# Strassen's scheme in the second matmul of a feed-forward network: seven block products in place of eight

## The chip, the cores and the metric

The kernel runs on one core of a Trainium2 chip. It is timed in device microseconds (us) for one whole execution; less is better. A core has TensorE (PE, matmuls out of the on-chip memory SBUF into the accumulators of PSUM), VectorE (DVE), ScalarE (ACT), GpSimd (POOL) and a queue, SP, that issues the DMAs here. Each engine works through its own list of instructions in the listed order and waits for the others by semaphores.

## The reference

One encoder layer on 2048 tokens of width 1024, in float32. The change concerns its last third:

```python
x = x + rms_norm(mix, g_post_mix)
h = rms_norm(x, g_pre_ffn)
f = jnp.square(jax.nn.relu(h @ w_ff1)) @ w_ff2      # 1024 -> 4096 -> 1024
return x + rms_norm(f, g_post_ffn)
```

## The kernel before

Three stages follow each other: the input projection, attention with the gating unit, and `stage3` (L889), which holds the output projection and the feed-forward network. Matmuls keep float32 accuracy by a split of every operand into a high part (`wh`, `fh`, `hh`, made by ACT) and a rest (`wl`, `fl`, `hl`, made by DVE as operand minus high part); `mm3` (L90 to L94) then takes three matmuls for one product: high by rest, rest by high, high by high. `split_sbuf` (L50 to L60) is the pair of instructions for a source in SBUF: ACT writes `hi` (L59, or L56 with a gain), DVE reads source and `hi` from SBUF and writes `lo` (L60, or L57 with the gain).

The network runs in two halves of 1024 tokens. A half goes through eight groups `g` of 512 hidden units. For a group, `ff1_unit` (L935) makes two of the group's four 128-unit blocks at a time, for both 512-token parts: PE sums over eight pieces of `w1` into four PSUM banks `f0` to `f3`; ACT takes the relu out of PSUM (L954), POOL squares it (L955), ACT and DVE split it into `fh` and `fl` (L59, L60). Then `ff2` (in `stage3`) multiplies the four blocks with the group's eight pieces of `w2` (4 rows of 128 by 2 columns of 512). It takes four PSUM banks at a time, each a 128-token by 512-column part of the result, sums four products of 128 hidden units into each, and DVE adds the bank to the sum `acc` in SBUF (L1083; ACT copies it in a half's first group, L1081). In the last group `done` adds the residual and writes out.

All weight halves share a pool of eight buffers `wh` and eight `wl` (`c.wp`): `w2` pieces take the place of `w1` pieces that FF1 has used, and `w1` pieces for the next group take the place of used `w2` pieces. Raw weights arrive through three buffers `wraw`. PSUM has six banks for products (`pm`) and two for transposes.

Outside the output projection (which is listed by hand, `in_order`) the order on each engine is made by the framework's scheduler when the kernel is built: it plans with its own estimates, and the engines then follow that list.

Of the kernel before, what the change touches and what calls it, by code (L numbers as in the profile page):

```python
# [9 lines left out]
F32 = mybir.dt.float32  # L10
F32R = mybir.dt.float32r
# [78 lines left out]
def mm3(nc, out, lh, ll, rh, rl, start=False, stop=False):  # L90

    nc.tensor.matmul(out, lhsT=lh, rhs=rl, start=start, stop=False)  # L92
    nc.tensor.matmul(out, lhsT=ll, rhs=rh, start=False, stop=False)  # L93
    nc.tensor.matmul(out, lhsT=lh, rhs=rh, start=False, stop=stop)  # L94
# [794 lines left out]
def stage3(tc, c, a, out):  # L889
# [4 lines left out]
    with ExitStack() as ctx:  # L894
        cst = ctx.enter_context(tc.tile_pool(name="s3c", bufs=1))
        hp = ctx.enter_context(tc.tile_pool(name="s3h", bufs=1))
        wk = ctx.enter_context(tc.tile_pool(name="s3k", bufs=2))
        sm = ctx.enter_context(tc.tile_pool(name="s3s", bufs=4))
        pm = ctx.enter_context(tc.tile_pool(name="s3p", bufs=6, space=PSUM))
# [4 lines left out]
        x1d = [dr.tile([1024, D], F32, name=f"x1d{e}", tag=f"x1d{e}") for e in range(2)]  # L904
# [8 lines left out]

        def normed(x1, out):
            rs = meansq(x1)
            nc.scalar.activation(out, x1, AF.Copy, scale=rs)
# [10 lines left out]
        def new_h():  # L927
            hh = hp.tile([P, 8, 1024], F32R, name="hh3", tag="hh3")
            hl = hp.tile([P, 8, 1024], F32R, name="hl3", tag="hl3")
            return hh, hl  # L930

        h = new_h()
        fpa = ctx.enter_context(tc.tile_pool(name="s3f", bufs=2))

        def ff1_unit(h, ws, c0, es, fs, pool):  # L935

            hh, hl = h
            bs = [pm.tile([P, 512], F32, name=f"f{m}", tag="mm3") for m in range(2 * len(es))]
            for kc in range(8):
                wh, wl = ws[kc]  # L940
                for m, b in enumerate(bs):
                    k, e = divmod(m, len(es))
                    cs = slice(c0 + k * P, c0 + (k + 1) * P)
                    ts = slice(es[e] * 512, (es[e] + 1) * 512)
                    mm3(nc, b, wh[:, cs], wl[:, cs], hh[:, kc, ts], hl[:, kc, ts], kc == 0, kc == 7)
                yield
            for k in range(2):
                if len(fs) == k:
                    fs.append(tuple(pool.tile([P, 1024], F32R, name=x, tag=x) for x in ("fh", "fl")))
                fh, fl = fs[k]  # L950
                for e in range(len(es)):
                    ts = slice(es[e] * 512, (es[e] + 1) * 512)
                    sq = wk.tile([P, 512], F32, name="sq", tag="sq")
                    nc.scalar.activation(sq, bs[k * len(es) + e], AF.Relu)  # L954
                    nc.gpsimd.tensor_tensor(sq, sq, sq, ALU.mult)  # L955
                    split_sbuf(nc, sq, fh[:, ts], fl[:, ts])

        def load2(g):
            return [[piece(nc, c, w2[(4 * g + k) * P:(4 * g + k + 1) * P, n * 512:(n + 1) * 512]) for k in range(4)]
                    for n in range(2)]  # L960

        with ExitStack() as octx:
# [9 lines left out]
            def load_x(i):  # L972
                xt = wk.tile([P, D], F32, name="xt3", tag="xt3", bufs=3)
                nc.sync.dma_start(xt, x2[i * P:(i + 1) * P, :])
                return xt
# [14 lines left out]
            raws, ws0, fs0, fs1 = [], [], [], []  # L990
            early = {7: 3, 8: 3, 9: 3, 11: 3, 12: 2, 13: 2, 14: 2}
            for i in range(18):
                old = 0 <= i - 1 < 16
                if 0 <= i - 3 < 8:
                    turned(xs[i - 3], h[0], h[1], i - 3)
                if i + 1 < 16:
                    halves(i + 1)
                if 0 <= i - 2 < 16:
                    nc.sync.dma_start(x1d[(i - 2) // 8][((i - 2) % 8) * P:((i - 2) % 8 + 1) * P, :], parts[i - 2])
                    if i - 2 < 8:  # L1000
                        rs2 = meansq(parts[i - 2])
# [6 lines left out]
                if i in (7, 11):  # L1008
                    unit = ff1_unit(h, ws0, 0, (i // 11,), fs0, fpa)
                for n in range(2):  # L1010
# [12 lines left out]
                    if 0 <= i - 2 < 8 and n == 1:  # L1023
# [14 lines left out]
        v0 = load2(0)  # L1038
        fpb = ctx.enter_context(tc.tile_pool(name="s3g", bufs=2))
        for _ in ff1_unit(h, ws0, 256, (0, 1), fs1, fpb):  # L1040
            pass

        gpost = bcast_row(nc, cst, a["g_post_ffn"][0:1], D, "gpost", "gain")
        with ExitStack() as fctx:
            ap_ = fctx.enter_context(tc.tile_pool(name="s3a", bufs=1, side="right"))

# [4 lines left out]
            def ff1(h, ws):  # L1051
                fs = []
                for pr, pool in enumerate((fpa, fpb)):
                    two = []
                    for _ in ff1_unit(h, ws, 2 * pr * P, (0, 1), two, pool):
                        pass
                    fs += two
                return fs

            def ff2(fs, ws, acc, first, last, done):  # L1060
                groups = [[(n, 4 * q + m) for m in range(4)] for n in range(2) for q in range(2)]
                if last:
                    groups = [[(n, m) for m in range(2) for n in range(2)]] + [[(n, m) for n in range(2)] for m in range(2, 8)]
                for grp in groups:
# [165 lines left out]
```

## Time and profile before

| | |
|---|---|
| median of three runs | 2489.77 us (2485.67 to 2494.03) |
| the profiled execution's own time | 2489.89 us |
| its span, first to last instruction | 2488.1 us |
| PE, DVE, ACT, POOL busy | 96%, 43%, 38%, 19% of the span |
| instructions of PE, DVE, ACT, POOL | 11591, 2262, 2069, 521 |
| feed-forward network alone | about 1100 to 2480 us, PE busy in every slice |

In the profile a group of instructions is given with its line, engine, operation, output and inputs, the shape and the count. A row of the timeline gives start, duration (of the whole row, where it merges several), engine, line, operation and, in brackets, how long the engine was idle before it and what ended that. A busy span of PE counts a matmul until its modelled end, so starts are compared with starts here.

### The profile page before, as it was taken

To read this page: it belongs to the slowest core of one execution; us is meant where nothing else is said; L and a number is where in the kernel's file an instruction comes from. 1 tells how busy PE (TensorE), PEld (TensorE's weight loads), DVE (VectorE), ACT (ScalarE), POOL (GpSimd) and SP (SyncE) were. 2 spreads that over 40 slices of the span, in tenths; PEclk is the share of its full clock that TensorE was granted. 3 is DMA by queue.
4 is the path that set the end of the run, shared out by engine and by line. 5 is a ranking of instruction groups with operands and counts; after the bars stand their busy time and mean duration, and the time that the engine had idled before them with its cause. 6 is when DMAs were issued, how large, how long until landed. Compare 5 with 4: busy or idle time off the path is not lost.

```text
span 2488.1 us, 31513 instructions
## 1 busy us (share of the span) xinstructions
PE 2385.7 (96%) x11591; PEld 1993.2 (80%) x11591; DVE 1072.5 (43%) x2262; ACT 934.0 (38%) x2069; POOL 463.3 (19%) x521
## 2 busy tenths in 40 slices
PE   7999999998889997899999999999999999999998
PEld 6787887887778876788888888888788888888887
DVE  5433523577766644751332332233622233223226
ACT  4424422377767774532221222123533122212212
POOL 4103102533222222320010011001211001001101
PEclk9999999999989998999999999999999999999999
DMA  7646365888867567761111111111611111111113
GB/s 271 218 140 203 119 188 160 216 199 191 197 170 179 144 173 223 228 230 38 58 46 46 55 52 49 37 60 57 206 55 47 46 56 51 47 39 55 47 47 118
DMA packets 213886, 296.13 MB, mean 119 GB/s; under 512 B 37090, under 2 KB 120549, under 8 KB 210661
## 3 DMA queue, kind: packets, MB, share of 16 engines
q1 hardware_dynamic: 188196, 280.23, 37.4%
q10 hardware_dynamic: 22976, 9.71, 1.5%
q0 software_dynamic: 2560, 4.20, 1.2%
q8 instruction: 91, 1.49, 0.3%
q14 instruction: 63, 0.51, 0.1%
HBM read 216.04 MB, written 82.74 MB: 120 GB/s over the span
## 4 chain that ended last, share of the span: by engine, by line
PE 64%; DMA 7%; DVE 3%; ACT 3%; POOL 1%; issue 1%; ACTq 0%; SPq 0%; DVEq 0%; POOLq 0%
PE f L92 10%; PE f L93 10%; PE f L94 10%; PE g L94 8%; PE g L93 8%; PE g L92 8%; PE t L599 1%; PE o L628 1%; PE o L627 1%; DMA yd<-x1b 1%; PE s L515 1%; DMA x1b<-stb 1%; PE s L516 1%; DMA od<-av 1%; PE mo L92 1%
## 5 line engine op out<-in xcount | busy, mean ns | idle before, releaser
L92 PE MATMUL g<-wl,fh 128*128 128x512 f32 x1024 | 398.8, 389 | 0.0
L94 PE MATMUL g<-wh,fh 128*128 128x512 f32 x1024 | 398.6, 389 | 0.0
L93 PE MATMUL g<-wh,fl 128*128 128x512 f32 x1024 | 398.6, 389 | 0.0
L93 PE MATMUL f<-hh,wl 128*128 128x512 f32 x1024 | 398.5, 389 | 0.0
L94 PE MATMUL f<-hh,wh 128*128 128x512 f32 x1024 | 398.5, 389 | 0.0
L92 PE MATMUL f<-hl,wh 128*128 128x512 f32 x1024 | 398.3, 389 | 0.0
L955 POOL TENSOR_TENSOR sq<-sq 128x512 f32<-128x512 f32 x128 | 132.0, 1051 | 1158.0 <-ACT sq L954 1142.8
L56 ACT ACTIVATE wh<-wraw,gain 128x512 fp32r<-128x512 f32 x200 | 143.3, 724 | 519.3 <-PE g L94 423.2
L57 DVE SCALAR_TENSOR_TENSOR wl<-wraw,gain,wh 128x512 fp32r<-128x512 f32 x200 | 157.7, 796 | 273.5 <-ACT wh L56 271.0
L60 DVE TENSOR_TENSOR fl<-sq,fh 128x512 fp32r<-128x512 f32 x128 | 99.5, 777 | 385.8 <-ACT fh L59 377.0
L93 PEld LDWEIGHTS f<-hh,wl 128*128 128x128 f32 x1024 | 192.2, 188 | 40.1
L92 PEld LDWEIGHTS f<-hl,wh 128*128 128x128 f32 x1024 | 192.2, 188 | 40.0
L94 PEld LDWEIGHTS f<-hh,wh 128*128 128x128 f32 x1024 | 192.2, 188 | 40.0
L93 PEld LDWEIGHTS g<-wh,fl 128*128 128x128 f32 x1024 | 192.3, 188 | 39.8
L94 PEld LDWEIGHTS g<-wh,fh 128*128 128x128 f32 x1024 | 192.2, 188 | 39.8
L92 PEld LDWEIGHTS g<-wl,fh 128*128 128x128 f32 x1024 | 192.2, 188 | 39.6
L1083 DVE TENSOR_TENSOR acc<-g,acc 128x512 f32<-128x512 f32 x192 | 127.3, 688 | 165.1 <-PE g L94 165.1
L588 ACT ACTIVATE p<-p,m 128x256 f32<-128x256 f32 (+2 forms) x384 | 173.9, 458 | 32.8 <-DVE m L558 15.7
L954 ACT ACTIVATE sq<-f 128x512 f32<-128x512 f32 x128 | 74.8, 597 | 285.4 <-PE f L94 278.4
L60 DVE TENSOR_TENSOR wl<-wraw,wh 128x512 fp32r<-128x512 f32 x136 | 93.9, 691 | 166.4 <-ACT wh L59 165.2
L59 ACT CAST wh<-wraw 128x512 fp32r<-128x512 f32 x136 | 84.6, 622 | 179.3 <-PE f L94 167.4
L532 DVE CUSTOM_DVE_ANT_0 p<-s,bias 128x256 f32<-128x256 f32 (+2 forms) x384 | 121.3, 356 | 44.3 <-PE s L516 31.6
(166 smaller groups left out, 4169.1 us busy)
## 6 DMA issues: line engine op xcount, KB each, us to landing
wraw<-in_w_ff_dram SPq DMA_DIRECT2D x256, 256.0 KB, 2.7
wraw<-in_w_in_dram SPq DMA_DIRECT2D x72, 256.0 KB, 2.9
xt<-in_x_dram SPq DMA_DIRECT2D x32, 512.0 KB, 6.6
v<-vd SPq DMA_DIRECT2D x40, 256.0 KB, 6.0
v<-vd SPq DMA_DIRECT2D x8, 1088.0 KB, 6.5
hd<-ht ACTq DMA_DIRECT2D x16, 512.0 KB, 4.7
vd<-vt SPq DMA_DIRECT2D x16, 512.0 KB, 3.1
qd<-e SPq DMA_DIRECT2D x32, 256.0 KB, 2.8
```

The source lines that it names most:

```text
L56: nc.scalar.activation(hi, src, AF.Copy, scale=scale)
L57: nc.vector.scalar_tensor_tensor(lo, src, scale, f32(hi), ALU.mult, ALU.subtract)
L59: nc.scalar.copy(hi, src)
L60: nc.vector.tensor_tensor(lo, src, f32(hi), ALU.subtract)
L92: nc.tensor.matmul(out, lhsT=lh, rhs=rl, start=start, stop=False)
L93: nc.tensor.matmul(out, lhsT=ll, rhs=rh, start=False, stop=False)
L94: nc.tensor.matmul(out, lhsT=lh, rhs=rh, start=False, stop=stop)
L532: nc.vector.tensor_tensor_reduce(po, so, bo, -1.0, 1e38, ALU.add, ALU.min, o.nm[:, br, cc:cc + 1])
L588: nc.scalar.activation(p[:, at + lo:at + hi], p[:, at + lo:at + hi], AF.Exp, bias=o.m[:, br, cc:cc + 1], scale=-1.0, accum_out=o.dn[:, br, ...
L954: nc.scalar.activation(sq, bs[k * len(es) + e], AF.Relu)
L955: nc.gpsimd.tensor_tensor(sq, sq, sq, ALU.mult)
L1083: nc.vector.tensor_tensor(av, b, av, ALU.add)
```

## The change

Only the network changes. Tokens go in four passes of 512 (`ps`) in place of two halves of 1024, and within a group of 512 hidden units the second matmul is done by Strassen's scheme in Winograd's form. The 512 tokens are two blocks of 256, the 1024 output columns two blocks of 512, the 512 hidden units two blocks of 256 (each as two parts `p` of 128). Seven products stand where eight block products stood; each is made for two token tiles `m` and takes two parts of three matmuls. So a group has 14 units of 6 matmuls, 84 matmuls for 512 tokens, where the kernel before has 192 for 1024. Over the run the second matmul has 2688 matmuls, before 3072; the first has 3072 in both.

What is new beside the products:

- `squares` (POOL): the relu stays in one buffer for each hidden block and is squared in two instructions of 128x256.
- `operands`: for each part, four POOL instructions on 128x256 make the sums of token blocks (`s1`, `s2`, and two in place), and seven splits (ACT L59, DVE L60, 128x256) make `fh1` to `fh7` and `fl1` to `fl7`.
- `load2`, `differences`, `second2`: `w2` comes in rows of 1024 columns (512 KB); eight POOL instructions on 128x512 make the differences of column blocks, and 14 splits of 128x512 make the weights of the products (before 8). The weights of products 1, 2, 6 and 5 have a pool of their own (`w2p`); those of 7, 3 and 4 go into `c.wp`.
- `CHAIN`: products 6, 7 and 4 go on summing into the bank `k=1` of product 1, product 3 into the bank of product 5. Between two of them DVE has to add the bank's present sum to a part of `acc` (L1154): 14 additions a group for 512 tokens, before 16 for 1024. `mm3` passes on a flag for banks that are continued.
- Each group of `w1` and `w2` is loaded and split once a pass, so four times instead of twice.

```diff
+        def squares(b, m, raw):
+            raw[m] = fp.tile([P, 512], F32, name="rf", tag=f"rf{m}")
+            nc.scalar.activation(raw[m], b, AF.Relu)
+            for e in range(2):
+                sl = raw[m][:, 256 * e:256 * e + 256]
+                nc.gpsimd.tensor_tensor(sl, sl, sl, ALU.mult)
...
+        def differences(raws):
+            ts = []
+            for r1, r2 in raws:
+                t1 = fp.tile([P, 512], F32, name="t1", tag="t1", bufs=2)
+                t2 = fp.tile([P, 512], F32, name="t2", tag="t2", bufs=2)
+                nc.gpsimd.tensor_tensor(t1, r1[:, 512:], r1[:, :512], ALU.subtract)
+                nc.gpsimd.tensor_tensor(t2, r2[:, 512:], t1, ALU.subtract)
+                nc.gpsimd.tensor_tensor(r1[:, 512:], r2[:, 512:], r1[:, 512:], ALU.subtract)
...
+            def operands(raw, p, fs):
+                a11, a21 = raw[p][:, :256], raw[p][:, 256:]
+                a12, a22 = raw[p + 2][:, :256], raw[p + 2][:, 256:]
...
+                nc.gpsimd.tensor_tensor(s1, a21, a22, ALU.add)
+                nc.gpsimd.tensor_tensor(s2, s1, a11, ALU.subtract)
+                op(1, a11)
+                op(2, a12)
+                op(6, s2)
+                op(5, s1)
+                nc.gpsimd.tensor_tensor(a21, a11, a21, ALU.subtract)
+                op(7, a21)
+                nc.gpsimd.tensor_tensor(a12, a12, s2, ALU.subtract)
+                op(3, a12)
+                op(4, a22)
...
+            CHAIN = ((1, 1, 0, 0, True, True, False), (2, 0, 0, 0, True, False, True), (6, 1, 0, 1, False, True, False),
+                     (5, 2, 1, 1, True, True, False), (7, 1, 1, 1, False, False, True),
+                     (3, 2, 0, 1, False, False, True), (4, 1, 1, 0, False, True, True))
...
+                order = [(x, m) for x in CHAIN for m in range(2)]
                 if last:
+                    order.sort(key=lambda x: x[1])
+                for j, ((n, k, r, q, opens, one, end), m) in enumerate(order):
+                    b = banks[k][m]
+                    ts = slice(m * P, (m + 1) * P)
+                    for p in range(2):
+                        fh, fl = fs[n, p]
+                        mm3(nc, b, fh[:, ts], fl[:, ts], *ws[n, p], opens and p == 0, p == 1, not opens)
+                    i = m + 2 * r
+                    av = acc[:, i, q * 512:(q + 1) * 512]
+                    if first and one:
+                        nc.scalar.copy(av, b)
+                    else:
+                        nc.vector.tensor_tensor(av, b, av, ALU.add)
...
                 for g in range(NG):
+                    first2(v, w2s)
+                    if not ps == g == 0:
+                        for _ in ff1_first(h, ws, raw):
+                            pass
+                        for _ in ff1_one(h, ws, 2, raw):
+                            pass
+                    operands(raw, 0, fs)
+                    for _ in ff1_one(h, ws, 3, raw):
+                        pass
+                    operands(raw, 1, fs)
...
+                    second2(v, w2s)
+                    if not last or ps < 3:
                         ws = load1((g + 1) % NG)
...
+                    ff2(fs, w2s, acc, g == 0, last, done, between)
```

How the scheduler lists these on the engines is shown at three places, all in one group (pass 1, fifth group) where the first matmul ends and the products begin. 24 of the 32 groups are listed like this; the last group of a pass differs only from the last row of the second place on (its products are ordered by token tile, and the very last group has no `w1` left to split), the first group of a pass somewhat more (ACT copies the banks of products 1, 6 and 5).

ACT before, at the end of a group's first matmul (`f2`, `f3` are banks, `sq` the relu of one):

```order
L59 CAST wh_14473<-wraw_14471 128x512
L954 ACTIVATE sq_14715<-f2_14603 128x512
L954 ACTIVATE sq_14720<-f3_14604 128x512
L59 CAST fh_14713<-sq_14715 128x512
L59 CAST fh_14713<-sq_14720 128x512
L56 ACTIVATE wh_14727<-wraw_14725,gain_95 128x512
```

ACT of the change at the same place (`rf_16178` is the relu of block 2, `rf_16241` that of block 3; `w2r` is raw `w2`):

```order
L59 CAST fh3_16208<-rf_16178 128x256
L59 CAST wh_16285<-w2r_16049 128x512
L59 CAST wh_16289<-w2r_16047 128x512
L59 CAST wh_16293<-w2r_16051 128x512
L59 CAST wh_16297<-w2r_16047 128x512
L59 CAST wh_16301<-w2r_16051 128x512
L937 ACTIVATE rf_16241<-f3_16216 128x512
L56 ACTIVATE wh_16307<-wraw_16305,gain_95 128x512
L59 CAST fh2_16253<-rf_16241 128x256
L59 CAST fh4_16275<-rf_16241 128x256
L59 CAST fh5_16261<-s1_16245 128x256
L59 CAST fh6_16257<-s2_16246 128x256
```

Before, the two relus stand next to each other, and no weight stands between them. Now the relu of block 3 stands behind the last operand of block 2 (`fh3`) and five casts of `w2`.

DVE before, from the last splits of a group to the first additions (`g0` to `g3` are the banks of the second matmul):

```order
L60 TENSOR_TENSOR fl_14714<-sq_14715,fh_14713 128x512
L60 TENSOR_TENSOR fl_14714<-sq_14720,fh_14713 128x512
L1083 TENSOR_TENSOR acc3_11316<-g0_14773,acc3_11316 128x512
L1083 TENSOR_TENSOR acc3_11316<-g1_14774,acc3_11316 128x512
L1083 TENSOR_TENSOR acc3_11316<-g2_14775,acc3_11316 128x512
```

DVE of the change, from the last `w2` rest to the additions of product 1 (`g10` is its bank for token tile 0, `g11` for tile 1):

```order
L60 TENSOR_TENSOR wl_16302<-w2r_16051,wh_16301 128x512
L1154 TENSOR_TENSOR acc3_14396<-g10_16355,acc3_14396 128x512
L60 TENSOR_TENSOR fl2_16254<-rf_16241,fh2_16253 128x256
L60 TENSOR_TENSOR fl5_16262<-s1_16245,fh5_16261 128x256
L60 TENSOR_TENSOR fl6_16258<-s2_16246,fh6_16257 128x256
L60 TENSOR_TENSOR fl7_16267<-rf_16149,fh7_16266 128x256
L60 TENSOR_TENSOR fl4_16276<-rf_16241,fh4_16275 128x256
L57 SCALAR_TENSOR_TENSOR wl_16308<-wraw_16305,gain_95,wh_16307 128x512
L60 TENSOR_TENSOR fl3_16272<-rf_16241,fh3_16271 128x256
L57 SCALAR_TENSOR_TENSOR wl_16314<-wraw_16311,gain_95,wh_16313 128x512
L1154 TENSOR_TENSOR acc3_14396<-g11_16356,acc3_14396 128x512
```

Before, the additions follow the splits at once, and nothing of the same group stands between two of them. Now six operands of block 3 and two `w1` rests stand between the additions of product 1's two banks.

POOL before has only the squares in a group. POOL of the change at this place (`t1`, `t2` are differences of `w2` for the next group):

```order
L983 TENSOR_TENSOR t1_16465<-w2r_16457 128x512
L940 TENSOR_TENSOR rf_16241<-rf_16241 128x256 x2
L1094 TENSOR_TENSOR s1_16245<-rf_16149,rf_16241 128x256
L1095 TENSOR_TENSOR s2_16246<-s1_16245,rf_16149 128x256
L1100 TENSOR_TENSOR rf_16149<-rf_16149 128x256
L984 TENSOR_TENSOR t2_16466<-w2r_16459,t1_16465 128x512
L1102 TENSOR_TENSOR rf_16241<-rf_16241,s2_16246 128x256
L985 TENSOR_TENSOR w2r_16457<-w2r_16459,w2r_16457 128x512
L983 TENSOR_TENSOR t1_16470<-w2r_16461 128x512
L984 TENSOR_TENSOR t2_16471<-w2r_16463,t1_16470 128x512
L985 TENSOR_TENSOR w2r_16461<-w2r_16463,w2r_16461 128x512
```

Between the squares of block 3 and its last operand (L1102) stand three sums of token blocks and one difference of `w2`; three more differences follow.

## Rows read from the trace of the kernel before

**Rows 1.** The page: PE with the other engines, and the granted clock in slices.
```profile
PE 2385.7 (96%) x11591; PEld 1993.2 (80%) x11591; DVE 1072.5 (43%) x2262; ACT 934.0 (38%) x2069; POOL 463.3 (19%) x521
...
PEclk9999999999989998999999999999999999999999
```
**Rows 2.** Stretches: length, busy of PE, PEld, DVE, ACT, POOL (instructions), clock, DMA.
```profile
1300.00:1400.00 100.00, 100.00 (x443) 82.81 (x442) 33.95 (x50) 23.04 (x36) 8.24 (x8) 1.00 0.16 50
```
**Rows 3.** Groups by line: busy in all, mean ns of one, idle before.
```profile
L94 PE MATMUL g<-wh,fh 128*128 128x512 f32 x1024 | 398.6, 389 | 0.0
...
L1083 DVE TENSOR_TENSOR acc<-g,acc 128x512 f32<-128x512 f32 x192 | 127.3, 688 | 165.1 <-PE g L94 165.1
```
**Rows 4.** Timeline of the network, PE, ACT and POOL around the relu and squares.
```profile
1352.44 0.39 PE L94 MATMUL f<-hh,wh 128*128 128x512 f32 x1
1352.67 0.39 PE L92 MATMUL f<-hl,wh 128*128 128x512 f32 x1
1352.87 1.28 ACT L954 ACTIVATE sq<-f 128x512 f32<-128x512 f32 x2 [18.99 <-PE f L94]
1353.55 2.04 POOL L955 TENSOR_TENSOR sq<-sq 128x512 f32<-128x512 f32 x2 [59.36 <-ACT sq L954]
...
1358.98 0.62 ACT L59 CAST fh<-sq 128x512 fp32r<-128x512 f32 x1 [0.38 <-POOL sq L955]
1359.50 0.62 ACT L59 CAST wh<-wraw 128x512 fp32r<-128x512 f32 x1
```
**Rows 5.** Timeline, DVE and ACT: instructions that follow each other, and 128x256 ones.
```profile
1026.10 0.73 ACT L59 CAST mh<-fa 128x256 fp32r<-128x256 f32 x2
1026.97 0.75 DVE L60 TENSOR_TENSOR ml<-fa,mh 128x256 fp32r<-128x256 f32 x2
...
1309.96 0.74 DVE L57 SCALAR_TENSOR_TENSOR wl<-wraw,gain,wh 128x512 fp32r<-128x512 f32 x1
1310.62 1.88 DVE L1083 TENSOR_TENSOR acc<-g,acc 128x512 f32<-128x512 f32 x3
```
**Rows 6.** Timeline, POOL and DVE, alone and at the same time.
```profile
313.85 1.29 POOL L139 TENSOR_TENSOR xl<-fr,xh 128x512 fp32r<-128x512 f32 x1
...
1001.49 1.27 DVE L1021 SCALAR_TENSOR_TENSOR r<-r,rs,gmix 128x1024 f32<-128x1024 f32 x1
1002.80 1.23 DVE L1022 TENSOR_TENSOR r<-r,xt 128x1024 f32<-128x1024 f32 x1
...
1012.05 3.50 POOL L886 TENSOR_TENSOR fa<-fa,fd 128x512 f32<-128x512 f32 x2
1012.12 2.29 DVE L1021 SCALAR_TENSOR_TENSOR r<-r,rs,gmix 128x1024 f32<-128x1024 f32 x1 [1.97 <-POOL rs L99]
1014.44 2.19 DVE L1022 TENSOR_TENSOR r<-r,xt 128x1024 f32<-128x1024 f32 x1
...
477.79 1.28 POOL L139 TENSOR_TENSOR xl<-fr,xh 128x512 fp32r<-128x512 f32 x1
477.90 1.21 DVE L558 TENSOR_TENSOR m<-m,nm 128x16 f32<-128x16 f32 x1
...
458.89 1.29 POOL L139 TENSOR_TENSOR xl<-fr,xh 128x512 fp32r<-128x512 f32 x1
459.48 0.69 DVE L716 SCALAR_TENSOR_TENSOR fs<-f,fs 128x512 f32<-128x512 f32 x1 [0.85 <-DMA fs<-sd]
```
**Rows 7.** DMA issues in the network: count, size, median us to landing.
```profile
xf<-x1d SPq DMA_DIRECT2D x15, 512.0 KB, 3.6
```
**Rows 8.** PE after idle time in the output projection, and a stretch of it (columns as Rows 2).
```profile
1046.83 1.96 PE L923 MATMUL tp<-ident,xt 128*128 128x128 f32 x8 [2.39 <-ACT xt L1024]
1048.45 0.78 PE L92 MATMUL mo<-qs,mh 128*128 128x512 f32 x1
...
1050.30 0.40 PE L93 MATMUL mo<-qs,ml 128*128 128x512 f32 x1
...
1048.00:1050.50 2.50, 2.50 (x9) 2.11 (x8) 1.74 (x4) 2.23 (x5) 0.00 (x0) 0.54 0.90 354
```

More of the change, by code (lines that the diff above doesn't have):

```diff
@@ L903, in stage3, with rows @@
         c.rp, c.rtag, c.nraw = wk, "wraw", 3
-        x1d = [dr.tile([1024, D], F32, name=f"x1d{e}", tag=f"x1d{e}") for e in range(2)]
+        x1d = [dr.tile([512, D], F32, name=f"x1d{e}", tag=f"x1d{e}") for e in range(4)]
+        def rows(i):
+            return x1d[i // 4][i % 4 * P:(i % 4 + 1) * P, :]
         def meansq(src):
@@ new lines, in ff2 @@
+            def ff2(fs, ws, acc, first, last, done, between):
+                banks = [[pm.tile([P, 512], F32, name=f"g{k}{m}", tag="mm3") for m in range(2)] for k in range(3)]
+                order = [(x, m) for x in CHAIN for m in range(2)]
+                if last:
+                    order.sort(key=lambda x: x[1])
+                for j, ((n, k, r, q, opens, one, end), m) in enumerate(order):
+                    b = banks[k][m]
+                    ts = slice(m * P, (m + 1) * P)
+                    for p in range(2):
+                        fh, fl = fs[n, p]
[6 more added lines that the diff above has]
+                        nc.vector.tensor_tensor(av, b, av, ALU.add)
+                    if last and end:
+                        done(i, q, av)
+                    between(j)
@@ L1132, in stage3, with between @@
[L1132 to L1133 removed]
+                    def between(j):
+                        if not last:
+                            return
+                        if ps < 3:
+                            if j in (1, 2, 4, 5):
+                                i = (1, 2, 4, 5).index(j)
+                                turned(nx[i], hn[0], hn[1], i)
+                        if j in (3, 4, 9, 10):
+                            residual((0, 2, 1, 3)[(3, 4, 9, 10).index(j)])
@@ L1136, in onehot, with between @@
+                    if last and ps < 3:
+                        hn = new_h()
+                    if last and ps == 3:
+                        for i in range(4):
+                            residual(i)
+                        def between(j):
+                            pass
+                    ff2(fs, w2s, acc, g == 0, last, done, between)
+                if ps < 3:
+                    h = hn
 def onehot():
```

222 lines of the change are left out of this document (114 added, 108 removed).

## The prediction

> **What bounds the kernel now.** I read the page's busy shares first, then a stretch inside the network, then the timeline there. PE is busy 96% of the span at a granted clock near full [rows 1]. In the network it is busy for the whole stretch: 443 matmuls in 100 us, 0.2257 us from start to start, while DVE has 34 us of work, ACT 23 and POOL 8 [rows 2]. So there every matmul taken out is worth 0.2257 us, as long as the other engines stay hidden. What to see in the timeline is how they hide: the relu starts 0.2 us after PE has begun on the next bank, and POOL starts 0.08 us after the relu's result [rows 4]; nothing in this chain is waited for, because the squares have a whole bank's time ahead of them.
>
> **What the change removes.** 3072 matmuls of the second product become 2688 (before: three groups of 1024, one of them in [rows 3]); 384 x 0.2257 = 86.7 us. The profiled execution took 2489.89 us, within 0.2 us of the median of the runs. With everything hidden the change gives 2489.9 - 86.7 = 2403.2 us.
>
> **What it adds.** Per group PE has 96 + 84 = 180 matmuls, 40.6 us. Start to start, in trains, DVE needs 0.66 us for a rest with gain (1310.62 - 1309.96), 0.61 for an addition (three in 1.88; one alone has 0.69 [rows 3]) and 0.35 for a 128x256 rest (two in 0.75) [rows 5]. A group has 8 rests of `w1`, 14 of `w2` (0.61), 14 of operands and 14 additions: 5.3 + 8.5 + 4.9 + 8.5 = 27.2 us. ACT has 8 + 14 + 14 splits and 4 relus, some 18 us at 0.52 for 128x512 (1359.50 - 1358.98 [rows 4]) and 0.36 for 128x256 (two in 0.73 [rows 5]). POOL has 8 squares of 128x256 at 0.51 (half of 1.02; two take 2.04 [rows 4]), 8 sums of 128x256 at 0.65 (half of the 1.29 of a 128x512 one [rows 6]) and 8 differences of 128x512 at 1.25: 19.3 us. No engine is full. The loads double, w1 and w2 four times instead of twice, 134 MB in the network; spread over 1300 us that is some 100 GB/s, and the DMA share of 0.16 at 50 GB/s [rows 2] would be about 0.3. I cost it at nothing, since each load is issued several microseconds before its use, with one exception below. The output projection keeps its order and loses 24 matmuls and four tiles of transposes to the network, where they are counted; nothing.
>
> What costs is order. Follow one group from the first matmul of block 3, t = 0; its 24 matmuls end at 5.42, and the 14 units of 1.354 follow. PE needs block 3's part of product 2 (`fl2`) at 8.8, and the fifth unit, product 6 of tile 0, starts at 10.8. The sixth, product 6 of tile 1, should start at 12.19. It continues the bank of product 1, so it waits for the addition of that bank, which DVE has behind all six operands of block 3 and two `w1` rests.
>
> How long those take depends on what POOL and DVE do to each other. In the trace a DVE instruction with two SBUF inputs that takes 1.27 and 1.23 us alone takes 2.29 and 2.19 beside two POOL instructions, which take 3.50 in place of 2.5; one of 16 columns takes 1.21 us because it starts just after a POOL instruction and ends with it. One that reads PSUM is untouched, 0.69 [rows 6]. The first two could be read as a shared rate, the third only as turns: the later one stands until the earlier is through, and of two that queue they alternate. The Trainium skill (SBUF — State Buffer, Who interferes with whom) has it as an exclusive lock, for a DVE instruction with two SBUF inputs against a GpSimd one that reads SBUF. By that rule the sum is the one of turns below; read as a shared rate, the rows give the first rival.
>
> In turns, then, by these durations:
> - Relu of block 2 at 0.2 to 0.8, squares 0.88 to 1.90. Then alternately one `w2` rest and four operand rests of DVE with `s1`, `s2` and two in-place sums of POOL (0.61 + 4 x 0.35 + 4 x 0.65): the last sum is done at 6.2, its cast `fh3` at 6.6.
> - ACT has five `w2` casts to do before block 3's relu: from 6.55, 5 x 0.52, so the relu runs from 9.15 to 9.75. Its bank was ready at 5.6.
> - From there on, what must pass before the addition of product 1's second bank, all by turns: POOL 2 squares, 4 sums and 4 differences of `w2` (1.0 + 2.6 + 5.0 = 8.6), DVE what is left of three `w2` rests, six operand rests, two `w1` rests and the addition (1.7 + 2.1 + 1.3 + 0.65 = 5.8). 9.8 + 14.4 = 24.2.
> - Of those, `fl2` is through at 13.5, so PE stands 4.7 us there, and 7.3 us before the sixth unit: 24.2 - 12.2 = **12.0 us lost a group**. Afterwards DVE alternates additions with rests of 0.61; the last unit needs an addition that is done at 34.7 and would start at 35.1: no further loss. The next group's `w1` is split 5 us before it is needed.
>
> The exception among the loads: the second `w2` difference needs 512 KB whose buffer comes free at 11.4; 3.6 us to land [rows 7] makes 15.0, and POOL's turn comes at 15.5. Hidden by 0.5 us.
>
> In the first group of a pass the two copies of product 1 are ACT's and don't stand behind the `w1` rests: `fh3` at 18.2, a `w2` cast and two of `w1` (about 2.1), two copies of 0.6, so 21.5 and 9.3 us lost. The last groups of a pass I take as 12. Sum: 28 x 12.0 + 4 x 9.3 = 373 us.
>
> The clock: after 2.39 us without a matmul the trace shows a stretch with a granted clock of 0.54, so nearly all of it at 1.2 GHz, the lower of the two levels; four matmuls took 1050.30 - 1048.45 = 1.85 us, 0.93 more than at full clock [rows 8]. The 7.3 us gap would bring that at least, 32 x 0.93 = 30 us; at the lower end it hides in DVE's later additions. I take half, 15 us. The Trainium skill (TensorE: Matmul & The Clock Gate, Part 1) has a clock gate that falls to half rate when PE is idle; by it the fall comes in every group and the full 30 us count.
>
> Total 2403.2 + 373 + 15 = **2791 us**.
>
> Bounds: POOL's 128x256 sums are not in the trace; half of 1.29 is the floor, and if the three differences behind block 3's last operand get no turn in between, 3.75 us less a group, 2671 us. If the `w2` load lands 2 us later, 2 us more a group, 2855.
>
> **Rivals.**
> - *Shared rate, no turns.* POOL by 3.5/2.5 = 1.4, DVE by 2.29/1.27 = 1.8: squares and sums of block 2 end at 6.0, relu of block 3 at 9.55, block 3's POOL work (4.9 x 1.4 = 6.8) at 16.4, cast, rest, `w1` rest and addition (0.45 + 0.65 + 1.2 + 0.65) at 19.4: 7.2 us a group, 2403 + 230 = 2633 us. For it: two of the three pairs; against it: the 16-column one.
> - *No interference.* The same chain with durations alone: 4.5, relu at 8.1, POOL 13.0, addition 15.3: 3.1 us, 2502 us. Against it: all the pairs but the PSUM one [rows 6].
> - *The other side: block 3's relu isn't held.* If ACT is through with the five casts when the bank is ready at 5.6, the chain is relu, POOL 4.9, cast, rest, rest, addition: done at 13.3, 1.1 us a group, 2440 us. It decides for faster when the addition is done by 12.19 + 86.7/32 = 14.9. For it: DVE, ACT and POOL have 13 us and more a group to spare. Against: block 2's POOL work alone, 0.88 + 3.6, ends at 4.5 without any interference, and five casts behind it end at 7.5.
> - *Worse.* Turns and late `w2` loads, or a clock that stays low: 2855 us and over.
>
> That the products are not saved I exclude: 2688 are listed.
>
> **Numbers.** Turns 0.62; shared rate 0.19; no interference 0.07; relu not held 0.05; worse 0.07. The predicted time is 2791 us. The range leaves out the two cheap rivals and the worst end: 2560 to 2850 us. 0.3% or 7.5 us is about what a measurement can tell. Faster: the relu's case, 0.05. Within 0.3%: part of the case without interference, 0.03. Slower: 0.92.
>
> **What would show it.** Right: in each group PE idle twice, before `fl2` (near 5 us) and before the first matmul of product 6 on `g11` (near 7 us), both ended by DVE; 443 matmuls per 100 us falling to about 342 (180 in 52.6 us); the relu L937 of `f3` starting some 3.5 us after its bank is full; L60 and L57 longer than 0.69 and 0.75 us where L983 to L985 run. Wrong: PE idle under 3 us a group, or ended by another than DVE; L60 at 128x256 near 0.4 us beside POOL (then no turns); idle at the start of the first matmul of a group (then `w1`, not the additions).

## The result, and the profile after

The changed kernel takes 2797.65 us (median of 4 runs, 2790.99 to 2801.22), the kernel before 2488.44 us beside it (2485.67 to 2494.03): a ratio of 1.1236, 95% interval 1.1205 to 1.1268. The forecast was 2791 us. The profiled execution took 2790.99 us, span 2789.0.

The page of the changed kernel, the lines that answer to [rows 1]; a part of its groups by line (busy in all, mean ns of one, idle before and its releaser) follows:

```profile
PE 2452.9 (88%) x11207; PEld 2002.8 (72%) x11207; DVE 1850.3 (66%) x3222; ACT 1285.5 (46%) x2837; POOL 1134.3 (41%) x1161
...
PEclk9999999999999998998998998899889899989989
...
L60 DVE TENSOR_TENSOR fl<-rf,fh 128x256 fp32r<-128x256 f32 x320 | 262.0, 837 | 254.1 <-ACT fh L59 254.1
...
L57 DVE SCALAR_TENSOR_TENSOR wl<-wraw,gain,wh 128x512 fp32r<-128x512 f32 x328 | 309.5, 956 | 99.8 <-ACT wh L56 96.9
...
L1154 DVE TENSOR_TENSOR acc<-g,acc 128x512 f32<-128x512 f32 x416 | 271.5, 680 | 43.8 <-PE g L94 41.4
```

384 matmuls are gone (11591 to 11207), and no engine is full: DVE has 66%, POOL 41%. What to see is the mean of a rest: 128x256 has become 837 ns, where two took 0.75 us before [rows 5], while the addition, which reads PSUM, has its 680 ns as before (688 [rows 3]). A stretch of the network, columns as in [rows 2]:

```profile
1300.00:1400.00 100.00, 85.17 (x329) 67.79 (x328) 71.40 (x95) 38.54 (x72) 43.87 (x42) 0.88 0.24 79
```

329 matmuls in 100 us in place of 443. And what PE waited for in the network (idle time in all, how often, the longest):

```profile
PE g L92 <- DVE acc L1154: 98.9, 31, 4.4
PE g L92 <- ACT fh L59: 75.6, 31, 5.9
PE g L93 <- DVE fl L60: 42.8, 28, 2.3
```

So nearly every one of the 32 groups has the two waits of the forecast, the first in two pieces. One group in the timeline, engine by engine; its t = 0 (first matmul of block 3) is 1619.90:

```profile
1619.90 0.39 PE L92 MATMUL f<-hl,wh 128*128 128x512 f32 x1
...
1625.34 0.39 PE L92 MATMUL g<-wl,fh 128*128 128x512 f32 x1
...
1630.86 0.50 PE L92 MATMUL g<-wl,fh 128*128 128x512 f32 x1 [1.96 <-ACT fh L59]
1632.92 0.80 PE L93 MATMUL g<-wh,fl 128*128 128x512 f32 x1 [1.56 <-DVE fl L60]
1633.52 0.63 PE L94 MATMUL g<-wh,fh 128*128 128x512 f32 x1
1633.94 0.63 PE L92 MATMUL g<-wl,fh 128*128 128x512 f32 x1
...
1642.33 0.79 PE L92 MATMUL g<-wl,fh 128*128 128x512 f32 x1 [3.39 <-DVE acc L1154]
...
1626.09 2.70 ACT L59 CAST wh<-w2r 128x512 fp32r<-128x512 f32 x5
1628.69 0.58 ACT L937 ACTIVATE rf<-f 128x512 f32<-128x512 f32 x1
...
1629.36 2.03 POOL L940 TENSOR_TENSOR rf<-rf 128x256 f32<-128x256 f32 x2 [1.88 <-ACT rf L937]
...
1638.01 1.72 POOL L983 TENSOR_TENSOR t<-w2r 128x512 f32<-128x512 f32 x1
1639.80 1.32 POOL L984 TENSOR_TENSOR t<-w2r,t 128x512 f32<-128x512 f32 x1
1641.09 1.71 POOL L985 TENSOR_TENSOR w2r<-w2r 128x512 f32<-128x512 f32 x1
...
1636.82 1.77 DVE L57 SCALAR_TENSOR_TENSOR wl<-wraw,gain,wh 128x512 fp32r<-128x512 f32 x1
1638.51 1.49 DVE L60 TENSOR_TENSOR fl<-rf,fh 128x256 fp32r<-128x256 f32 x1
1639.93 1.75 DVE L57 SCALAR_TENSOR_TENSOR wl<-wraw,gain,wh 128x512 fp32r<-128x512 f32 x1
1641.60 2.47 DVE L1154 TENSOR_TENSOR acc<-g,acc 128x512 f32<-128x512 f32 x4
```

Products begin at 1625.34. The five `w2` casts stand ahead of block 3's relu, which runs at t = 8.8. Three DVE rests (1636.82 to 1641.60) are each stretched to 1.49 to 1.77 us by the POOL difference that they meet. The ends of the two engines' instructions alternate: a rest at 1638.59, a difference at 1639.73, a rest at 1640.00, a difference at 1641.12, a rest at 1641.68, a difference at 1642.80. The steps are 1.14, 0.27, 1.12, 0.56 and 1.12 us, and each is a little under what that instruction takes alone: these are turns.

After the first wait PE runs at the lower of its two clock levels: 0.42 us from 1633.52 to 1633.94. Product 6 of tile 1 starts at t = 22.4 (1642.33), behind the first of the four additions that begin at 1641.60. The fifth difference since the relu, at 1641.09, runs beside that addition, which reads PSUM. The text on the listing of GpSimd above counts three differences behind block 3's last operand; the listing itself has four.

### The profile page after: what moved, and what is told of

It is laid out like the page before. It is cut to its first block, busy times and chain, and to the rows that moved or that the text cites. A ratio compares the mean times of both kernels' runs of the same rounds, so it can differ in the third digit from the quotient of the medians.

```text
span 2789.0 us, 33978 instructions
## 1 busy us (share of the span) xinstructions
PE 2452.9 (88%) x11207; PEld 2002.8 (72%) x11207; DVE 1850.3 (66%) x3222; ACT 1285.5 (46%) x2837; POOL 1134.3 (41%) x1161
## 5 line engine op out<-in xcount | busy, mean ns | idle before, releaser
L92 PE MATMUL g<-wl,fh 128*128 128x512 f32 x896 | 408.2, 457 | 193.9 <-DVE acc L1154 98.9
L60 DVE TENSOR_TENSOR fl<-rf,fh 128x256 fp32r<-128x256 f32 x320 | 262.0, 837 | 254.1 <-ACT fh L59 254.1
L940 POOL TENSOR_TENSOR rf<-rf 128x256 f32<-128x256 f32 x256 | 189.5, 765 | 587.7 <-ACT rf L937 587.7
L57 DVE SCALAR_TENSOR_TENSOR wl<-wraw,gain,wh 128x512 fp32r<-128x512 f32 x328 | 309.5, 956 | 99.8 <-ACT wh L56 96.9
L56 ACT ACTIVATE wh<-wraw,gain 128x512 fp32r<-128x512 f32 x328 | 232.5, 721 | 273.7 <-DMA wraw<-in_w_ff_dram 119.6
L60 DVE TENSOR_TENSOR wl<-w2r,wh 128x512 fp32r<-128x512 f32 x320 | 267.2, 868 | 111.7 <-ACT wh L59 111.4
L1154 DVE TENSOR_TENSOR acc<-g,acc 128x512 f32<-128x512 f32 x416 | 271.5, 680 | 43.8 <-PE g L94 41.4
L94 PEld LDWEIGHTS g<-wh,fh 128*128 128x128 f32 x896 | 198.8, 222 | 45.1
L937 ACT ACTIVATE rf<-f 128x512 f32<-128x512 f32 x128 | 75.8, 594 | 284.0 <-PE f L94 281.4
L59 ACT CAST fh<-rf 128x256 fp32r<-128x256 f32 x320 | 126.4, 406 | 154.6 <-POOL rf L940 76.3
L59 ACT CAST wh<-w2r 128x512 fp32r<-128x512 f32 x320 | 177.5, 616 | 8.5 <-PE mo L94 2.2
```

The lines of the kernel that those rows point to most:

```text
L56: nc.scalar.activation(hi, src, AF.Copy, scale=scale)
L57: nc.vector.scalar_tensor_tensor(lo, src, scale, f32(hi), ALU.mult, ALU.subtract)
L59: nc.scalar.copy(hi, src)
L60: nc.vector.tensor_tensor(lo, src, f32(hi), ALU.subtract)
L937: nc.scalar.activation(raw[m], b, AF.Relu)
L940: nc.gpsimd.tensor_tensor(sl, sl, sl, ALU.mult)
```

## The experiments

All are the changed kernel with the edit shown. "Period" is the median distance from one group's first product matmul to the next group's, read from the timeline; it is 53.5 us in the changed kernel.

| | median, us | ratio to before, 95% interval | period, us |
|---|---|---|---|
| the change | 2797.65 | 1.1236 (1.1205 to 1.1268) | 53.5 |
| a_relu | 2656.56 | 1.0680 (1.0656 to 1.0705) | 48.0 |
| b_adds | 2622.25 | 1.0542 (1.0517 to 1.0568) | 46.4 |
| c_both | 2550.96 | 1.0253 (1.0224 to 1.0282) | 43.8 |
| d_allDVE | 2555.71 | 1.0276 (1.0249 to 1.0302) | 45.1 |
| e_memset | 2623.29 | 1.0559 (1.0542 to 1.0577) | 46.6 |
| f_fill | 2804.51 | 1.1275 (1.1258 to 1.1292) | 52.5 |
| g_direct | 2488.67 | 1.0012 (0.9998 to 1.0025) | 43.5 |
| h_allDVE2 | 2575.73 | 1.0363 (1.0337 to 1.0389) | 45.9 |
| i_spread | 2530.99 | 1.0177 (1.0145 to 1.0209) | 43.7 |
| j_squares | 2481.10 | 0.9984 (0.9972 to 0.9996) | 42.1 |
| k_stages | 2560.58 | 1.0292 (1.0264 to 1.0321) | 45.2 |
| l_stages2 | 2506.44 | 1.0092 (1.0073 to 1.0112) | 42.4 |

**The order on ScalarE and VectorE: a_relu, b_adds, c_both.**

```diff
 # a_relu and c_both: every cast of second2 stands behind the relu of block 3 on ACT
+start = len(tc.nc.cur_bb.bb.instructions)
 second2(v, w2s)
+following(tc, start, raw["relu"])     # order only, no wait
 # b_adds and c_both: written after unit 1 (product 1, tile 1), from between(1)
+sums = tc.nc.cur_bb.bb.instructions[-1]     # the addition of g11
+start = len(tc.nc.cur_bb.bb.instructions)
 second2(v, w2s)
 ws = load1((g + 1) % NG)
+following(tc, start, sums)
```

> Only the order on ScalarE changes: the relu of block 3 stands ahead of the w2 casts (six of them, one cast then follows it, five follow block 3's operands). Theory (turns between VectorE's two-input instructions and GpSimd): the relu runs about 2.5 us earlier in a group, at t = 6.6 instead of 9.1, but the scheduler now lists the w2 rests on VectorE behind block 3's operands and still ahead of product 1's additions; the same instructions have to pass by turns before the addition of its second bank (GpSimd 8.6 us, VectorE six w2 rests 3.7, six operand rests 2.1, two w1 rests 1.3, two additions 1.3), 7.2 + 17.0 = 24 us. So PE's wait before fl2 shrinks by about 2 us and the one before product 6 grows by as much: 2780 us, between 2750 and 2810. Rival (the held relu is the cause by itself): the whole chain moves 2.5 us forward, 28 x 2.5 = 70 us, 2728 us.

> Only the order on VectorE (and the order of writing) changes: the six splits of w2 for products 7, 3 and 4 and the splits of the next w1 are written behind product 1, and their rests are held behind the addition of product 1's second bank. The relu of block 3 is still behind five w2 casts. Theory (turns; a fixed amount of work of VectorE and GpSimd must pass before PE can go on): product 6 of tile 1 starts near t = 17.5 instead of 22.4 (t = 0 at the first matmul of block 3), but the eight rests then stand ahead of the additions of products 2 and 6, so that product 7, which continues product 6's bank, starts only near 28 (before 26.6): no gain, 2800 us, between 2760 and 2830. Rival (the place of that one addition is the cause): 28 x 4.9 = 137 us less, 2660 us.

> Both orders together: relu of block 3 first on ScalarE, and the additions of product 1 ahead of the eight weight rests on VectorE. Theory (turns): from the relu's end at 7.2 the work ahead of product 7 is GpSimd 8.6 us, VectorE 2.1 + 5.0 us and four additions 2.5 us, of which two hide beside GpSimd: product 7 starts near 25 instead of 26.6, and the time is some 1.5 to 3 us a group less, 2700 to 2760 us, 2730 us. Rival (order alone is the cause, the engines have room): with both places mended the waits go and the time is 2440 to 2500 us.

The theory missed all three: 141, 175 and 247 us less, where it allowed some 20, none and 70. It had taken the work that must pass by turns in the window as fixed, wherever it is listed. It isn't: what is moved out of the window isn't waited for. For a_relu and b_adds the rivals, at 2728 and 2660 us, were nearer than the theory, and still too dear. In a_relu POOL shows why (timeline, a group whose relu of block 3 starts at 1237.25):

```profile
1241.97 0.91 POOL L1112 TENSOR_TENSOR rf<-rf,s 128x256 f32<-128x256 f32 x1
1243.03 1.29 POOL L993 TENSOR_TENSOR t<-w2r 128x512 f32<-128x512 f32 x1
1249.16 1.27 POOL L994 TENSOR_TENSOR t<-w2r,t 128x512 f32<-128x512 f32 x1 [4.83 <-DMA w2r<-in_w_ff_dram]
```

The differences, still four ahead of the addition in the changed kernel, come behind block 3's last sum; all but the first wait for their load and miss the window. The edits are not pure changes of order on ACT and DVE: the scheduler also moved PE's list (product 5 ahead of 6 in a_relu; four matmuls of the next group's block 0 and 1 between products 5 and 7 in b_adds and c_both). "Order alone" (2440 to 2500 us) was not right for c_both either.

**Are the turns real: e_memset.**

```diff
-nc.gpsimd.tensor_tensor(t1, r1[:, 512:], r1[:, :512], ALU.subtract)
-nc.gpsimd.tensor_tensor(t2, r2[:, 512:], t1, ALU.subtract)
-nc.gpsimd.tensor_tensor(r1[:, 512:], r2[:, 512:], r1[:, 512:], ALU.subtract)
+for t in (t1, t2, r1[:, 512:]):      # and r2[:, :512] in second2
+    for n in (512, 512, 316):
+        nc.gpsimd.memset(t[:, :n], 0.0)
```

> The eight differences of w2 on GpSimd are replaced by memsets of the same tiles (two of 128x512 and one of 128x316, about 1.25 us together), so GpSimd is busy as long and at the same places, but reads nothing there; the products that use these tiles get zeros. Theory (turns of two-input instructions with instructions of GpSimd that read SBUF): the rests beside the former differences go back from 1.5 to 1.75 us to some 0.7, the addition of product 1's second bank is done near t = 18.3 instead of 22.4 in a group, 4 us less, 28 x 4.1 = 115 us and a little clock: 2675 us, between 2640 and 2710. Rival (GpSimd's queue: block 3's last sum stands behind a difference whatever it does): no change, 2797 us. Rival (any use of SBUF by GpSimd, writing too): no change, 2797 us, with rests as long as before.

174 us less, more than the theory's 122, against two rivals with no change. POOL is nearly as busy as before (1080.8 us over the run against 1134.3), but the rests beside it are short. In a group, DVE, PE and POOL:

```profile
1336.40 0.76 DVE L60 TENSOR_TENSOR fl<-rf,fh 128x256 fp32r<-128x256 f32 x2 [0.19 <-ACT fh L59]
1337.08 1.41 DVE L57 SCALAR_TENSOR_TENSOR wl<-wraw,gain,wh 128x512 fp32r<-128x512 f32 x2
1338.41 2.48 DVE L1157 TENSOR_TENSOR acc<-g,acc 128x512 f32<-128x512 f32 x4
...
1326.69 0.39 PE L92 MATMUL g<-wl,fh 128*128 128x512 f32 x1
...
1339.14 0.50 PE L92 MATMUL g<-wl,fh 128*128 128x512 f32 x1 [1.54 <-DVE acc L1157]
...
1335.01 0.92 POOL L1105 TENSOR_TENSOR rf<-rf,s 128x256 f32<-128x256 f32 x1
1335.87 1.54 POOL L979 MEMSET w2r<- 128x512 f32 x3
```

The same two `w1` rests took 1.77 and 1.75 us beside differences and take 1.41 together here, one of them beside a memset. (The row of three memsets is two of 128x512 and one of 128x316.) Two 128x256 rests beside these memsets take 0.76 together, where one took 1.49 beside a difference. So it is POOL's reading that makes a two-input DVE instruction wait, not POOL being busy. Product 6 of tile 1 starts 12.5 us after the group's first product matmul (1326.69 to 1339.14), 4.5 us earlier than in the changed kernel and near the 4.1 of the theory; the period falls by 6.9, so 2.4 us a group lie behind that restart. How much of the 174 us is the missing turns stays open: the memsets of `t1` and `t2` need no load, POOL has them earlier, and the stretch ahead of the addition holds 1.9 us of memsets where four differences ended and a fifth began. For the same reason the rival of GpSimd's queue is only partly tested: the queue got shorter there too. The Trainium skill (SBUF — State Buffer, Who interferes with whom) says just this: a GpSimd instruction that only writes does not contend with a VectorE one that has two SBUF inputs. The run agrees.

**Is the clock a cost of its own: f_fill.**

```diff
+for _ in range({2: 18, 5: 26}.get(j, 0)):     # ahead of units 2 and 5 of a group
+    nc.tensor.matmul(extra, lhsT=fs[1, 0][0][:, :P], rhs=ws[1, 0][0], start=True, stop=True)
```

> 44 matmuls more a group (except the last of a pass) that nobody needs, into a bank of the transposes: 18 ahead of product 2, 26 ahead of product 6 of tile 1, 9.9 us at full clock, placed where PE stood idle; the result is untouched. Theory (the chain on VectorE and GpSimd sets when product 6 of tile 1 starts, and the half clock before it only fills what would be idle): product 6 starts at the same time (t = 22.4), and only the half clock behind it goes, 1.4 to 2.8 us of a group's 4.2: 28 x 2 = 56 us less, 2740 us, between 2710 and 2770. Rival (the clock's 123 us come on top of the waits): 2797 - 115 = 2680 us. Rival (the extra matmuls aren't hidden): over 2850 us.

A stretch, and one of the waits:

```profile
1300.00:1400.00 100.00, 98.22 (x428) 79.40 (x427) 76.17 (x100) 42.55 (x80) 49.39 (x48) 1.00 0.24 79
```

```profile
PE g L92 <- DVE acc L1159: 16.4, 19, 0.9
```

One group, whose products begin at 1206.98, around the extra matmuls (`tp`) and the addition that product 6 of tile 1 waits for:

```profile
1206.98 0.39 PE L92 MATMUL g<-wl,fh 128*128 128x512 f32 x1
...
1217.87 6.05 PE L1150 MATMUL tp<-wh,fh 128*128 128x512 f32 x26
1223.80 0.50 PE L92 MATMUL g<-wl,fh 128*128 128x512 f32 x1
...
1223.07 0.68 DVE L1159 TENSOR_TENSOR acc<-g,acc 128x512 f32<-128x512 f32 x1
```

The clock is 1.00 in the stretch. Product 6 of tile 1 starts 16.82 us after the group's first product matmul (16.98 in the changed kernel), but that start alone says little: five units and the 44 extra matmuls, 0.2267 us each, last 16.8 us by themselves. What tells is the addition. It ends at 1223.75, 16.8 us after the first product matmul, and in the changed kernel at 1642.28, 16.9 after it. So with PE at full clock the chain on DVE and POOL ends when it did before: the theory's main point.

But nothing is won: 2804.51 us, 7 more, where 56 less were expected. At product 7 of tile 1, four units on, PE now waits some 1 us for an addition that it used to reach too late to notice, and the median period falls by 1.1 us only. Between the two profiled executions (2790.99 and 2798.46 us) the 24 middle groups gain 18 us together, but the first groups of the four passes take 20 more, and the network's first product matmul starts 6 us later (1092.63 in place of 1086.65). In the middle groups, then, full clock won 0.7 us a group; the rest of the half clock was idle time in another form.

**Do the passes cost: g_direct.**

```diff
-                operands: 14 splits of 128x256, sums; CHAIN: seven products
+                for k in range(4): split_sbuf(nc, raw[k], fh, fl)          # 128x512
+                for n in range(2):                                        # eight block products
+                    for k, m in [(k, m) for k in range(4) for m in range(4)]:
+                        mm3(nc, banks[m], fh[:, ts], fl[:, ts], *ws[n, k], k == 0, k == 3)
```

> The four passes of 512 tokens without the scheme: eight block products (96 matmuls a group), no sums, no differences, eight splits of w2 and four of 128x512 for the blocks, eight additions a group; loads of w1 and w2 four times as in the change. Theory (passes and loads cost nothing, the scheme's chain does): the matmuls of before, 2490 us, between 2475 and 2520. Rival (the passes, with twice the loads and weight splits, take a good part of the loss): 2600 us or more.

Right: 2488.67 us. Twice the loads and twice the weight splits cost nothing that can be measured; the loss is the scheme's.

**Nothing on GpSimd: d_allDVE, h_allDVE2, i_spread.**

```diff
 # all three
-nc.gpsimd.tensor_tensor(sl, sl, sl, ALU.mult)             # two of 128x256
+nc.scalar.activation(raw[m], raw[m], AF.Square)           # one of 128x512
-nc.gpsimd.tensor_tensor(s1, a21, a22, ALU.add)            # and all sums and differences
+nc.vector.tensor_tensor(s1, a21, a22, ALU.add)
+in_order(tc, start, ("DVE", "Activation"))                # h: and "SP"; i: and "PE"
 # h, i: three w1 loads ahead of the products; i: weights of 7 and 3 split among block 2's operands
```

> Nothing is left out. Squares go from GpSimd to ScalarE (one instruction of 128x512), all sums of token blocks and all differences of w2 from GpSimd to VectorE; so nothing takes turns. VectorE and ScalarE follow the written order in all groups but the last of a pass: relu, square and the operands of product 2 and 6 of block 3, additions of product 1, weights of 7, additions of 2 and 6, weights of 3, additions of 5, weights of 4, and so on. VectorE then has 27.2 + 8 x 0.35 + 8 x 0.61 = 34.9 us of the 40.6 us of a group. Theory (turns were the cause): every instruction is in time in the 28 groups in order, PE has no wait there, and only the first and last groups of a pass lose some 5 us each: 2403 + 8 x 5 = 2445 us, between 2410 and 2480, faster than the kernel before. Rival (VectorE is full: it becomes the bound, since 35 of 40.6 us can't be packed): 1 to 4 us lost a group, 2480 to 2570 us. Rival (something in the scheme itself, such as continued banks or the loads, costs): near 2700 us still.

> The version with nothing on GpSimd (2556 us), with one thing changed: the order of the loads is fixed too, three pieces of the next w1 are loaded ahead of a group's products and the others as their buffers come free, so that the four loads of the next w2 no longer stand ahead of w1's in the queue. In the run before, PE waited for w1's splits, whose loads were issued behind w2's, and VectorE had idle time there and was late afterwards. Theory: the 28 groups fall from 45 us to between 41 and 42.5, the edges of the passes stay: 2403 + 24 + 28 x 1 = 2455 us, between 2435 and 2490. Rival (VectorE is the bound: 35 us of work and its waits for casts don't fit): the wait moves to the additions and the time stays over 2520 us.

> The version with nothing on GpSimd, work spread differently: the weights of products 7 and 3 are split among the operands of block 2 (where ScalarE and VectorE wait for each other) instead of behind product 1 and 6, the last differences of w2 come right behind the first ones, the first loads of the next w2 are issued behind product 1 and the others behind product 5, and TensorE too follows the written order in all groups but the last of a pass. Theory (VectorE's work fits; what PE waited for, the addition of product 5 and the first split of w1, was only behind work that could stand elsewhere): the groups fall from 45 us to between 41 and 42, 2403 + 24 + 28 x 0.8 = 2450 us, between 2430 and 2475, so faster than before. Rival (VectorE is the bound: 35 us and its waits for casts fill a group): still 43.5 us a group or more, 2510 us or over.

All three miss: 2556, 2576 and 2531 us. No rest is lengthened any more, but DVE and ACT, bound to a written order, wait for each other's results (below, ACT for DVE's sum `rf`), and the old fault comes back. PE's largest wait in i_spread, a stretch, and ACT:

```profile
PE g L92 <- ACT fh L59: 57.3, 27, 5.3
...
1300.00:1400.00 100.00, 95.65 (x412) 77.82 (x411) 83.36 (x154) 54.05 (x105) 0.00 (x0) 0.98 0.28 95
...
1318.09 0.62 ACT L59 CAST wh<-w2r 128x512 fp32r<-128x512 f32 x1
1319.80 0.71 ACT L59 CAST fh<-rf 128x256 fp32r<-128x256 f32 x2 [1.09 <-DVE rf L1101]
1320.42 0.59 ACT L937 ACTIVATE rf<-f 128x512 f32<-128x512 f32 x1
```

Block 3's last matmul had started at 1315.99, and its relu stands behind block 2's last casts, 4 us late; PE waited 57.3 us for `fh` in 27 places. In h_allDVE2 PE waited 35.0 us for `w1`'s casts and 30.5 for additions, much as in d_allDVE: fixing the order of the loads was not the cure. All three times lie where the rival put them that has VectorE full (2480 to 2570, over 2520, 2510 or over). DVE has idle time left, 83% busy in the stretch, but whether its 35 us of work a group fit into 41 in any order is not shown.

**The parts put together: j_squares, k_stages, l_stages2.**

```diff
 # j_squares: c_both, squares on ACT, sums on DVE (as above); differences stay on POOL, scheduler's order
 # k_stages: the DVE rests of product 3 behind the addition of 6, those of 4 and w1 behind that of 5
+if j == 5: second2(v, w2s, (3,))
+if j == 7: second2(v, w2s, (4,)); ws = load1((g + 1) % NG)
 # l_stages2: load1 at j == 9 instead, behind the addition of 7
```

> As the version with both orders (2551 us), with the squares on ScalarE and the sums of token blocks on VectorE, so that only the differences of w2 (10 us a group) are left on GpSimd. Theory (turns): no GpSimd instruction stands any more between the relu of block 3 and its operands, and product 6's wait (0.8 us a group) goes; what is left is the wait for additions at the end of a group: 1 to 2 us less a group, 2551 - 28 x 1.5 = 2510 us, between 2490 and 2530. Rival (VectorE's 2.8 us more of sums take it back): 2550 us.

> As the version with squares on ScalarE, sums on VectorE and differences on GpSimd (2481 us), with the weight rests on VectorE in three stages: those of product 7 behind the additions of product 1, those of 3 behind the additions of product 6, those of 4 and of the next w1 behind the additions of product 5. In the version before, PE stood 1.1 us in every group ahead of a matmul of the next group's block 0, which waited for the addition of product 2, and that stood behind all eight rests. Theory (the addition, queued behind rests that nobody needs yet, was the last wait in a group): 28 x 1.1 = 31 us less, 2450 us, between 2440 and 2465. Rival (VectorE is full by now and the wait moves to the next addition): 2475 us or more.

> As the version in three stages (2561 us), with the rests of the next w1 on VectorE one stage later, behind the additions of product 7. In the version before, three w1 rests stood ahead of these additions and took 5.15 us in place of 2.1, since the differences of w2 on GpSimd, which start when the next w2 has arrived, fell beside them; product 4, which continues product 7's bank, waited 2.7 us in every group. Theory (turns, and a needed addition queued behind rests that are lengthened by them): with the additions ahead, product 4 doesn't wait, and the w1 rests, lengthened or not, are in time for the next group: 28 groups of 40.7 to 41.5 us, 2450 us, between 2435 and 2470. Rival (VectorE's list is full, the wait moves to the first pieces of w1 in the next group): over 2490 us.

j_squares is the one version with the scheme whose interval doesn't lie above 1: 2481.10 us, better than its forecast, though the gain on the kernel before, 0.16%, is within what counts as no change here. Which of its two moves off POOL, squares or sums, brought the 70 us from c_both was not tested apart. A stretch, and the largest of PE's waits:

```profile
1200.00:1300.00 100.00, 98.11 (x432) 80.61 (x431) 74.15 (x131) 49.83 (x98) 31.19 (x18) 1.00 0.28 95
```

```profile
PE f L101 <- DVE acc L1162: 20.0, 21, 1.0
```

A period of 42.1 us beats the 43.5 of g_direct, but the matmuls alone would take 40.8 (180 at 0.2267). Of the 78 us that are left over 2403, 24 x 1.25 = 30 lie in the middle groups, nearly all in that wait. The other 48 were not taken apart; where one pass ends and the next begins, the distance between two groups is 53.8 to 55.0 us, 47.1 in g_direct.

k_stages took the wait away where it was and got a worse one, product 4 on product 7's bank. DVE there:

```profile
1201.69 5.15 DVE L66 SCALAR_TENSOR_TENSOR wl<-wraw,gain,wh 128x512 fp32r<-128x512 f32 x3
1206.76 2.47 DVE L1163 TENSOR_TENSOR acc<-g,acc 128x512 f32<-128x512 f32 x4
1209.16 2.06 DVE L66 SCALAR_TENSOR_TENSOR wl<-wraw,gain,wh 128x512 fp32r<-128x512 f32 x3
```

Three `w1` rests take 5.15 us where the differences run, and 2.06 a little later. l_stages2 moved them behind the additions; then the next group's first matmuls wait for them. DVE, and beside it POOL's last two differences; below, PE's wait:

```profile
1213.25 3.46 DVE L66 SCALAR_TENSOR_TENSOR wl<-wraw,gain,wh 128x512 fp32r<-128x512 f32 x2
...
1212.27 3.90 POOL L1132 TENSOR_TENSOR w2r<-w2r,t 128x512 f32<-128x512 f32 x2 [4.48 <-DVE wl L69]
```

```profile
PE f L102 <- DVE wl L66: 39.1, 35, 2.5
```

In both, the wait moved to what a difference on POOL had lengthened. In l_stages2 it also moved where the rival with VectorE's list full had put it, at a time that the rival allowed (over 2490 us). Turns and a full list were not tested apart here.

## Why the prediction was right, point by point

- *384 matmuls, 86.7 us.* Right: 11207 are left, and a group's 96 first matmuls take 21.76 us, 0.2267 each. The 0.2257 of the forecast counts matmuls that only reach into the stretch; by 0.2267 the 384 are worth 87.0 us.
- *Loads and doubled weight work at nothing.* Right, by g_direct.
- *Block 3's relu held.* Forecast to run from 9.15 to 9.75, it ran from 8.8 to 9.4, behind the five casts named. Its part in the loss can't be had from a_relu alone, since PE's order moved too.
- *Two waits, both ended by DVE, near 5 and 7 us.* The places are right. The first measured 2.1 + 1.8 us beyond the matmuls' own spacing, its first half ended by ACT's cast `fh`. The second measured 3.5 to 4.5 us, not 7.3. Two things make it shorter. Product 6 restarts at 22.4 instead of 24.2. The ten POOL instructions of the forecast do pass before the addition, but the squares start at 9.5 instead of 9.8, and the turns behind them take 12.9 us instead of 14.4: a difference adds 1.12 to 1.14 us where 1.25 was put in, a `w1` rest 0.56 for 0.65, a 128x256 rest 0.27 for 0.35. And 9 to 13 matmuls between the waits are slowed, most to 0.43 us, 1.7 to 2.8 us in all: PE comes later to the same wait.
- *12.0 us lost a group.* At the restart 10.2 us are lost (16.98 against 6.80 after the first product matmul).
- *No further loss after the restart, and 15 us for the clock.* The first is the step that failed. From the restart on, 54 matmuls took 13.7 to 15.3 us in place of 12.2. From the first product matmul to the next group's first matmul the 24 middle groups take 31.43 us on average and lose 31.43 - 19.04 = 12.4, which is near the forecast's 12.0 + 0.5; but 1.8 us too many ahead of the restart stand against 2.2 us behind it, so that the sum comes out is partly luck: two errors cancel. f_fill parts the 2.2: at full clock 30.69 - 16.82 - 12.24 = 1.6 us of it stay, 1.0 of them a wait for an addition that DVE has behind others. Half clock alone gives 0.6 us a group, near the 0.5 put in; the later additions were the cost taken as nothing.
- *First and last groups of a pass.* 2791.0 - 2403.2 - 24 x 12.4 = 90 us for eight, forecast 4 x 9.3 + 4 x 12 = 85. Here too errors cancel: the first groups take 31.8 to 33.6 us for their 84 matmuls and so lose 12.7 to 14.5 each, 54 together where 37 were put in, which leaves 36 for the last groups in place of 48.
- *The rivals.* Turns against a shared rate is decided by the alternating ends in the group shown: by the shared rate a `w1` rest would take 0.74 x 1.8 = 1.3 us and a 128x256 rest 0.41 x 1.8 = 0.7, and they took 1.75 and 1.49; the restart at 22.4, against 24.2 by turns and 19.4 by the rate, agrees. e_memset doesn't part these two, since without reads neither lengthens anything; it speaks against the rival without interference. The rival on the other side was priced too cheaply: with block 3's relu not held a_relu takes 2656.56 us, not 2440. There the rests that the scheduler then lists ahead of product 1's addition, and the operands' own turns, stay; PE waited 99.9 us for additions in 25 places.

## What to carry to other kernels

A scheme that saves matmuls is paid in what must happen between two matmuls on other engines. Count not only their work (66% busy here) but what stands in their lists, at each point that PE waits for, ahead of the one instruction that it needs: reordering, with no work taken away (c_both; PE's list moved with it), gave back 247 of the 309 us. Keep GpSimd's reads of SBUF away from the stretches where VectorE has two-input work that is waited for, and expect that every wait removed uncovers the next one.

## What the runs showed of the hardware

- Memsets on GpSimd (two of 128x512 and one of 128x316 in 1.54 us) left VectorE's two-input rests beside them at their length: two of 128x256 took 0.76 us. Differences stretched three `w1` rests to 5.15 us where three took 2.06 without them (k_stages).
- GpSimd's differences and VectorE's two-input rests ended by turns, each 0.27 to 1.14 us after the other's end. Additions that read PSUM kept their length: 680 ns on average with GpSimd 41% busy, 688 with 19%.
- Behind PE waits such as 1.96, 1.56 and 3.39 us, 16 to 24 matmuls a middle group ran 0.43 us apart in place of 0.2267. With extra matmuls in the waits the granted clock of the stretch went from 0.88 to 1.00, and the time did not fall.
